# First queries and keys of heads 0 and 1 from the scale alone, with the shift added as a bias

## The chip, the cores and the metric

The kernel runs on one core of one Trainium2 chip, in one launch. The metric is the device time of that launch in microseconds (us). Three runs of the kernel before took 1315.22, 1316.06 and 1317.70 us; their median, 1316.06, is the time before.

## The reference, cut to what matters

Two layers of a diffusion backbone on 256 context tokens (`x_prompt`) and 1024 latent tokens (`x_sample`) of width 1024. Layer 0 mixes tokens by gated linear attention with 4 heads, layer 1 by softmax attention; the change touches only the beginning of layer 0:

```python
mod = silu(c) @ w_ada[0] + b_ada[0]          # c for latent tokens, c_ctx for context tokens
shift, scale, gate = split(mod, 3)            # 1024 each
h = rms_norm(x, norm_g[0]) * (1.0 + scale) + shift
proj = h @ gla_w_in                           # queries 512, keys 512, values 1024, gate 1024
q = q.reshape(..., 4 heads, 128) * 128 ** -0.5
z = (h @ wa1[d]) @ wa2[d] + ba[d]             # decay of direction d, rank 16
```

Since `h` is a scaled part plus `shift`, a product `h @ w` is the product of the scaled part plus one vector, `shift @ w`, that is the same for all latent tokens.

## The kernel before, in words

**Products and numbers.** The products of float32 numbers are made from pairs of float16 tiles: each operand is scaled by a power of two and split into a high and a low half, and three matmuls (high by high, low by high, high by low) are summed in a bank of PSUM (`mm3`, L126). A product over 1024 inputs takes eight blocks of 128, so 24 matmuls. `hT_hi` and `hT_lo` hold the modulated input with its 1024 channels as eight blocks of 128 partitions and its 1280 tokens along the free side; `whi` and `wlo` are the halves of a weight block.

**Tokens.** They come in three groups, in this order: latent tokens 0 to 511 (group 0), latent tokens 512 to 1023 (group 1), the 256 context tokens (group 2). `CHUNKS` and `GROUPS` name the same three in columns and in rows of 128.

**Set-up (L1218 to L1285).** It stands in the program in this order:
- `ada_load` (L274) loads blocks of `w_ada`, 1024 by 256 each, in two halves. Blocks 4 to 7 hold the scale, blocks 0 to 3 the shift. `gemv` (L278) multiplies a block by the condition vectors with 8 matmuls (L283), ScalarE copies the bank (L289), and `mod_sum` (L292) sums four blocks into `modT` (L303). The second four blocks land in the space of `hT_hi` and `hT_lo`, which is still free.
- `group(0)` loads the first four rows of x, squares them on ScalarE (L345) and scales them on VectorE (L348); `transpose` (L353) turns each of the eight channel blocks on TensorE, and VectorE copies them to `xT`.
- `load_qk` loads and splits the query and key weights of heads 0 and 1 (L145 is the load, into a `wst` tile).
- `affine` (L316) makes the gain `gs` and the shift `sh` with a power of two that fits both, and `inv_h`, its inverse. The power of two comes from `pow2`, which takes a maximum over all partitions by a transposing matmul (L89).
- `modulate` (L357) makes one tile of a group: ScalarE computes `h = gs*xT + sh` (L364), GpSimd rounds it to the high half (L365), VectorE subtracts for the low half (L366).
- `split_rank` (L394) scales and splits the rank weights `wa1` and `wa2`.
- For each of the three groups: load, normalise, transpose and modulate it (groups 1 and 2), then `qk_piece` (L450) for the queries and the keys of head 0, then `rank` (L430): 24 matmuls of 32 output rows (L438) that rotate through three column groups of TensorE, a copy (L443), a matmul that sums the three parts, and an eviction to `r`.

The value weights of head 0 are loaded and split after the last tile of group 1.

**The loop (`gla`, L664).** Five passes of ten slots, one slot for a token tile. In pass h a slot projects the values of head h and the output gate of head h-1, makes decays two slots ahead, and runs the products of the scan for head h; `intra`, `local` and `outer` are its parts. In head 0, `PIECES` places the queries and keys of head 1: those of group 0 in slots 4 (queries) and 5 (keys), the rest in slots 8 and 9. `filler` loads further `w_ada` blocks, one in each odd slot from slot 1, and multiplies them in the even slots; a list of jobs splits the next weights.

**The order.** Each engine runs its instructions in a fixed order. The scheduler that builds the program chooses it for each engine from a simulated timeline, from the dependences and the order of the source; `issue_after(x)` forbids an instruction to stand before x. Loads are issued by SyncE, whose queue holds at a load until the space of its target is free.

## Time and profile before

| | |
|---|---|
| median of three runs | 1316.06 us (1315.22 to 1317.70) |
| the profiled execution | 1315.01 us |
| its span, first to last instruction | 1313.2 us |
| TensorE matmul (PE) | 1224.5 us busy, 93% |
| TensorE weight load (PEld), beside PE | 796.7 us, 61% |
| VectorE (DVE) | 904.4 us, 69% |
| ScalarE (ACT) | 587.5 us, 45% |
| GpSimd (POOL) | 390.0 us, 30% |
| mean granted TensorE clock | 0.986 |
| memory read, written | 104.31 MB, 37.24 MB |

The span is what the profiler recorded of one execution; the execution's own time is 1.8 us longer. Busy shares are means over stages that differ: TensorE is at 93% over the whole, but the first fortieth of the span (33 us) is set-up, where it does little else than multiply `w_ada` blocks. In the lines of the profile, `A<-whi,cst` names the output and the inputs by the program's names; "[3.61 <-DMA whi<-in_w_ada]" after an instruction says how long its engine stood idle before it and what ended the wait. In a table of stretches each engine has its busy time and, in brackets, its count of instructions.

### The profile page before, as it was taken

The page shows a single profiled execution, that of the slowest core. Times are in us where ns is not written, and L with a number is a line of the kernel's source. Part 1 is how long each engine was busy: PE and PEld are TensorE (multiplying, and loading weights), DVE is VectorE, ACT ScalarE, POOL GpSimd, SP SyncE. Part 2 cuts the span into 40 slices and gives each one's busy share as a digit, 9 for nine tenths or more (in the row PEclk, how much of TensorE's full clock was granted, in tenths as well). Part 3 has the DMA queues.
Part 4 walks back from the last instruction along what each step waited for, and adds up shares of the span by engine and source line. Part 5 has one row for each costly group of instructions (what it writes and reads, how often), then busy time and mean ns, then how long its engine had stood idle before and what let it go on. Part 6 is the DMA issues. An engine that isn't in the chain of part 4 may idle for free. (4 is left out here: it accounts for less than half of the span.)

```text
span 1313.2 us, 22291 instructions
## 1 busy us (share of the span) xinstructions
PE 1224.5 (93%) x8107; PEld 796.7 (61%) x8107; DVE 904.4 (69%) x2072; ACT 587.5 (45%) x1431; POOL 390.0 (30%) x623
## 2 busy tenths in 40 slices
PE   4789999999999999897999998999999999989998
PEld 2347664655656556665777656767666766766444
DVE  1876768886877788746564568878657587775652
ACT  2565555655656566313343454454445454431110
POOL 2232122322422233401222544544233245423000
PEclk9899999999999999998999999999999999999999
DMA  9712555354445334678653278677947748968432
GB/s 299 244 64 70 170 184 181 111 179 146 135 145 162 108 117 144 209 179 256 148 152 108 66 181 141 135 135 138 201 93 166 149 89 143 192 134 201 175 136 79
DMA packets 344766, 199.11 MB, mean 152 GB/s; under 512 B 229406, under 2 KB 331534, under 8 KB 343376
## 3 DMA queue, kind: packets, MB, share of 16 engines
q1 hardware_dynamic: 297024, 159.67, 48.5%
q10 hardware_dynamic: 47312, 37.25, 9.1%
q8 instruction: 64, 1.05, 0.3%
q0 software_dynamic: 320, 0.77, 0.2%
q14 instruction: 46, 0.38, 0.1%
HBM read 104.31 MB, written 37.24 MB: 108 GB/s over the span
## 5 line engine op out<-in xcount | busy, mean ns | idle before, releaser
L131 PEld LDWEIGHTS <-hT_hi 128*128 128x128 f16 x1440 | 140.1, 98 | 97.8 <-issue 5.3
L131 PE MATMUL mm<-whi,hT_hi 128*128 128x512 f16 (+1 forms) x560 | 195.5, 349 | 2.6 <-DVE orsa L120 2.3
L131 PE MATMUL mm<-whi,hT_lo 128*128 128x512 f16 (+1 forms) x560 | 195.4, 349 | 0.0
L131 PE MATMUL mm<-wlo,hT_hi 128*128 128x512 f16 (+1 forms) x560 | 195.4, 349 | 0.0
L131 PEld LDWEIGHTS <-whi 128*128 128x128 f16 x1368 | 134.7, 99 | 81.0 <-issue 10.9
L131 PE MATMUL mm<-hT_hi,whi 128*128 128x256 f16 (+1 forms) x512 | 155.1, 305 | 6.0 <-POOL hT_hi L365 2.9
L1028 POOL TENSOR_SCALAR phl<-p,srec 128x1280 f16<-128x1280 f32 (+1 forms) x80 | 98.3, 1229 | 204.6 <-DVE srec L1023 91.1
L131 PE MATMUL mm<-hT_lo,whi 128*128 128x256 f16 (+1 forms) x512 | 155.5, 304 | 0.2 <-DVE hT_lo L366 0.2
L131 PE MATMUL mm<-hT_hi,wlo 128*128 128x256 f16 (+1 forms) x512 | 155.3, 304 | 0.0
L1029 DVE SCALAR_TENSOR_TENSOR phl<-p,srec,phl 128x1280 f16<-128x1280 f32 (+1 forms) x80 | 107.6, 1345 | 47.9 <-POOL phl L1028 47.6
L131 PE MATMUL mm<-PT,vh 128*128 128x256 f16 x672 | 117.6, 279 | 14.7 <-DMA PT<-phl 12.0
L999 PE MATMUL S<-kT,wst 128*128 128x512 f16 (+1 forms) x624 | 121.7, 338 | 3.8 <-ACT p L1007 3.3
L1002 DVE TENSOR_REDUCE smx<-S 128x1 f32<-128x1280 f32 (+1 forms) x80 | 101.4, 1269 | 17.8 <-PE S L999 17.5
L1007 ACT ACTIVATE p<-S,snb,sexp 128x1280 f32<-128x1280 f32 (+1 forms) x80 | 99.6, 1245 | 30.3 <-DVE phl L1029 11.4
L131 PEld LDWEIGHTS <-hT_lo 128*128 128x128 f16 x720 | 70.3, 98 | 50.3 <-issue 0.9
L131 PEld LDWEIGHTS <-wlo 128*128 128x128 f16 x720 | 70.9, 99 | 41.0 <-issue 2.9
L999 PEld LDWEIGHTS <-wst 128*128 128x128 f16 x624 | 61.0, 98 | 55.5 <-issue 4.6
L131 PE MATMUL mm<-PT,vl 128*128 128x256 f16 x336 | 93.9, 280 | 0.0
L131 PEld LDWEIGHTS <-vh 128*128 128x128 f16 x672 | 66.8, 100 | 27.5 <-issue 10.5
L131 PE MATMUL y<-whi,ogT 128*128 128x256 f16 (+1 forms) x336 | 75.0, 312 | 7.7 <-DVE xr L749 7.7
L1004 ACT ACTIVATE snb<-smx,nsexp 128x1 f32<-128x1 f32 x80 | 23.4, 293 | 130.2 <-DVE smx L1002 124.9
L153 DVE TENSOR_REDUCE wmx<-wst 128x1 f32<-128x512 f32 x104 | 64.7, 675 | 14.4 <-DMA wst<-in_gla_w_in 7.8
(337 smaller groups left out, 2552.2 us busy)
## 6 DMA issues: line engine op xcount, KB each, us to landing
wada<-in_w_ada SPq DMA_DIRECT2D x13, 1024.0 KB, 6.3
wst<-in_gla_w_in SPq DMA_DIRECT2D x12, 1024.0 KB
wst<-in_att_w_in SPq DMA_DIRECT2D x10, 1024.0 KB, 5.0
xr<-x_d SPq DMA_DIRECT2D x11, 512.0 KB
og_d<-gx ACTq DMA_DIRECT2D x40, 128.0 KB, 3.8
og_d<-og ACTq DMA_DIRECT2D x40, 128.0 KB, 2.9
wst<-og_d SPq DMA_DIRECT2D x5, 1024.0 KB
out<-xr ACTq DMA_DIRECT2D x17, 256.0 KB, 2.1
```

The costliest lines, as they stand in the source:

```text
L131: self.nc.tensor.matmul(out, a, b, start=k == 0 and j == 0, stop=k == n - 1 and j == 2)
L153: nc.vector.tensor_reduce(mx[:, j : j + 1], st[:, 2 * j : 2 * j + 2, :], AX.XY, ALU.max, apply_absolute_value=True)
L999: nc.tensor.matmul(S[:, a : a + n], x, y, start=m == 0, stop=m == 2)
L1002: last = nc.vector.tensor_reduce(mx, S, AX.X, ALU.max).ins
L1004: nc.scalar.activation(nb, mx, AF.Copy, scale=self.nsexp)
L1007: nc.scalar.activation(p, S, AF.Exp, scale=self.sexp, bias=nb, accum_out=den)
L1028: nc.gpsimd.tensor_scalar(hi, p, r, 2.0 ** 14, ALU.mult, ALU.mult)
L1029: nc.vector.scalar_tensor_tensor(lo, p, r2, hi, ALU.mult, ALU.subtract)
```

## The change

It reorders the set-up and adds a second way to make the first queries and keys.

- **Loads.** The first x group is loaded first, then the query and key weights of heads 0 and 1, then the scale blocks 4 to 7, then the shift blocks 0 to 3, two into `hT` columns 768 to 1280 and two into the space that scale blocks 4 and 5 leave.
- **Scale alone.** `affine_scale` makes a gain from the scale blocks only, with its own power of two. Group 0 is modulated with it, without a shift (`modulate` with `sh` None), and the queries and keys of heads 0 and 1 for group 0 are products of these tiles (`qk_sum`, four banks of 24 matmuls).
- **Shift as a bias.** `shift_bias` splits the shift and multiplies it with the query and key weights: 24 matmuls of 32 output rows by 512, a copy on ScalarE, four small matmuls. The evictions of the four banks add the result as a bias. Those of head 1 are kept in the tile `hold`, and GpSimd copies them to their place at slots 4 and 5 of head 0, where before they were computed.
- **Second modulation.** After the first tile pass the full gain and shift are made by `affine` as before; groups 1 and 2 use them, and group 0 is modulated a second time with them, since values, gates, rank and the later heads use the full tiles.
- **Rank.** `rank` is parted into `rank` and `rank_sum`, in the order group 1, group 0, group 2, with other banks.
- **Spaces.** The pool `ada` opens before the set-up, its first tile is `hold`, and so `filler` starts its loads at slot 7 instead of slot 1. `rows` and `wa2` take other buffers.
- **Order.** `issue_after` ties a few matmuls of the key and query products behind the small matmuls of `mod_sum`, `pow2` and `shift_bias`.

The core of the difference, with the two new functions:

```diff
+    def affine_scale(self):
+        nc = self.nc
+        g = self.t(self.p1, [P, KT, 2], F32, "ga")
+        self.gains(0, g)
+        mx = self.t(self.small, [P, 1], F32, "af_m", bufs=1)
+        nc.vector.tensor_reduce(mx, g, AX.XY, ALU.max, apply_absolute_value=True)
+        m2 = self.mulcol(mx, self.mhalf[:, 0:1], self.p1, "af_n", -64.0)
+        s, inv = self.pow2(m2)
...
+    def shift_bias(self, wq):
...
+        hi, lo = (c[:, j, :, 0:2] for j in range(2))
+        nc.scalar.activation(hi, sh, AF.Copy, scale=s)
+        nc.vector.scalar_tensor_tensor(lo, sh, s, hi, ALU.mult, ALU.subtract)
+        ps = self.bank("A")
+        for k in range(KT):
+            j = k % 4
+            for m, (x, y) in enumerate(((0, 0), (0, 1), (1, 0))):
+                last = nc.tensor.matmul(
+                    ps[32 * j : 32 * j + 32, :], c[:, x, k, :], wq[y][:, k, :], start=k < 4 and m == 0,
+                    stop=k >= 4 and m == 2, tile_position=(0, 32 * j), skip_group_check=True,
+                ).ins
+        m = self.t(self.hw, [P, 512], F32, "h32", bufs=3)
+        nc.scalar.copy(m, ps)
...
+        if self.sh is None:
+            last = nc.scalar.activation(h, xT, AF.Copy, scale=g)
...
+    def qk_piece(self, h, which, c, wq, ps=None, inv=None, bias=None):
+        if c == 0 and self.kept:
+            out = self.qkt[:, 1280 * which : 1280 * which + 512]
+            self.nc.gpsimd.tensor_copy(out, self.kept.pop(0))
...
+            xs = group(0)
+            wq = k.wtile(0)
+            for i in range(2):
+                run(k.load_qk(wq, 0, i))
...
+            k.mod_sum(parts, "cs")
+            k.gs, k.sh, k.inv_h = k.affine_scale()
             for kk in range(KT):
                 act, dve = k.modulate(xT[:, kk, :], kk, GROUPS[0][0])
...
+            with tc.issue_after(act.ins):
+                xs = group(1)
...
+            bias, b1, b2 = k.shift_bias(wq)
+            p1 = k.tick
+            pieces = [k.qk_sum(0, j, 0, wq, ties=({}, {3: m1, 11: p1, 20: b1})[j]) for j in range(2)]
...
+            for kk in range(KT):
+                act, dve = k.modulate(k.transpose(xs, kk, banks[1:][kk % 5]), kk, GROUPS[1][0])
+            pieces += [k.qk_sum(1, j, 0, wq, ("z", "mm")[j], ({3: b2}, None)[j]) for j in range(2)]
...
+            for kk in range(KT):
+                k.modulate(xT[:, kk, :], kk, GROUPS[0][0])
+            with tc.issue_after(act.ins):
+                xs = group(2)
...
-            elif queue:
+            elif queue and slot > 6:
```

**SyncE, the loads of the set-up.** In this queue before, after the small loads, the scale blocks (`whi`, `wlo`, x2 for the two halves of a block) stand ahead of the x rows, and the shift blocks (`hT_hi`, `hT_lo`) at the end, with a load of the loop's state behind them:

```order
L274 DMA whi_31_147<-in_w_ada 128x4x256 x2
L274 DMA wlo_32_148<-in_w_ada 128x4x256 x2
L274 DMA whi_37_175<-in_w_ada 128x4x256 x2
L274 DMA wlo_38_176<-in_w_ada 128x4x256 x2
L1237 DMA x_203<-in_x_sample 128x1024
L1237 DMA x_205<-in_x_sample 128x1024
L1237 DMA x_207<-in_x_sample 128x1024
L1237 DMA x_209<-in_x_sample 128x1024
L145 DMA wst_275<-in_gla_w_in 128x8x256
L145 DMA wst_304<-in_gla_w_in 128x8x256
L274 DMA hT_hi_71<-in_w_ada 128x4x256 x2
L274 DMA hT_lo_72<-in_w_ada 128x4x256 x2
```

And the same place after:

```order
L1319 DMA x_150<-in_x_sample 128x1024
L1319 DMA x_152<-in_x_sample 128x1024
L1319 DMA x_154<-in_x_sample 128x1024
L1319 DMA x_156<-in_x_sample 128x1024
L146 DMA wst_173<-in_gla_w_in 128x8x256
L146 DMA wst_202<-in_gla_w_in 128x8x256
L275 DMA whi_58_231<-in_w_ada 128x4x256 x2
L275 DMA wlo_59_232<-in_w_ada 128x4x256 x2
L275 DMA whi_60_237<-in_w_ada 128x4x256 x2
L275 DMA wlo_61_238<-in_w_ada 128x4x256 x2
L275 DMA hT_hi_71<-in_w_ada 128x4x256 x2
L275 DMA hT_lo_72<-in_w_ada 128x4x256 x2
```

The x rows and the query and key weights (`wst`) moved ahead of all of `w_ada`; the last two shift blocks, which follow the rows shown, go to `whi` and `wlo` of the first scale blocks.

**ScalarE, between the first tiles and those of group 1.** Before, the last tile of group 0 (`h` from `xT`) is followed by the squares of group 1 (`junk`), the evictions of head 0's first queries and keys (L457), the scaling of the rank weights (L403 to L410), the copy of the rank product (L443), and the first tile of group 1:

```order
L364 ACTIVATE h_110_465<-xT_224,sh_90_409,gs_89_405 128x512
L345 ACTIVATE junk_146,nt_s_136_600<-x_592 128x1024
L345 ACTIVATE junk_146,nt_s_136_600<-x_594 128x1024
L345 ACTIVATE junk_146,nt_s_136_600<-x_596 128x1024
L345 ACTIVATE junk_146,nt_s_136_600<-x_598 128x1024
L457 ACTIVATE qk_98<-mm_509,iqk_101_433 128x512
L457 ACTIVATE qk_98<-mm_535,iqk_102_435 128x512
L403 ACTIVATE wa1h_486<-wa_29_144,p2s_482 128x256
L407 ACTIVATE wa_21_128<-wa_28_142,p2s_482 98x1024
L410 ACTIVATE wa_21_128<-wa_28_142,p2s_482 1x1024
L443 COPY h_130_586<-mm_561 96x512
L364 ACTIVATE h_140_618<-z_613,sh_90_409,gs_89_405 128x512
```

After, from the last tile of the first pass on:

```order
L423 ACTIVATE h_98_406<-xT_247,gb_374 128x512
L402 ACTIVATE junk_149,nt_s_105_422<-x_414 128x1024
L402 ACTIVATE junk_149,nt_s_105_422<-x_416 128x1024
L289 COPY mod_477<-o_468 128x256
L402 ACTIVATE junk_149,nt_s_105_422<-x_418 128x1024
L402 ACTIVATE junk_149,nt_s_105_422<-x_420 128x1024
L385 ACTIVATE af_b_496<-modT_19_129 128x16
L349 ACTIVATE shc_531<-modT_19_129,p2s_527 128x8x2
L360 COPY h_138_560<-A_535 128x512
L425 ACTIVATE h_149_636<-cs_631,sh_118_493,gs_117_489 128x512
L534 ACTIVATE qk_98<-mm_575,qkb_141_569,iqa_99_410 128x512
L534 ACTIVATE qk_98<-mm_600,qkb_143_573,iqa_100_412 128x512
```

The copy of a shift block (L289), the small steps of `affine` and `shift_bias` (L385, L349) and the copy of the bias product (L360) now stand ahead of group 1's first tile; the rank weights went behind.

**TensorE, in the key product of group 0 (bank `mm_600`).** Before, the transposes of group 1's first row stand behind the whole key product (bank `mm_535`), whose last matmul is the first row here:

```order
L131 MATMUL mm_535<-hT_hi_71,wlo_60_274 128x512
L353 MATMUL z_613<-ident_79,x_592 128x128
L353 MATMUL cs_622<-ident_79,x_592 128x128
L353 MATMUL A_631<-ident_79,x_592 128x128
L353 MATMUL kt_640<-ident_79,x_592 128x128
L353 MATMUL U_649<-ident_79,x_592 128x128
```

After, eight transposes of all four rows and the two matmuls of `pow2` (L89) stand within it:

```order
L132 MATMUL mm_600<-hT_lo_72,whi_38_171 128x512
L410 MATMUL cs_631<-ident_79,x_414 128x128
L410 MATMUL U_658<-ident_79,x_414 128x128
L410 MATMUL cs_631<-ident_79,x_416 128x128
L410 MATMUL U_658<-ident_79,x_416 128x128
L410 MATMUL cs_631<-ident_79,x_418 128x128
L410 MATMUL U_658<-ident_79,x_418 128x128
L410 MATMUL cs_631<-ident_79,x_420 128x128
L410 MATMUL U_658<-ident_79,x_420 128x128
L89 LDWEIGHTS af_m_499
L89 MATMUL o_501<-ident_79,af_m_499 128x128
L89 LDWEIGHTS af_o_517
```

The key product of group 0 now waits in the queue for the normalised rows of group 1.

More of the change, by code (lines that the diff above doesn't have):

```diff
@@ L130, in mm3 @@
             for j, (a, b) in enumerate(((lh, rh), (lh, rl), (ll, rh))):
-                self.nc.tensor.matmul(out, a, b, start=k == 0 and j == 0, stop=k == n - 1 and j == 2)
+                with self.tc.issue_after(ties[3 * k + j]) if ties and 3 * k + j in ties else nullcontext():
+                    self.nc.tensor.matmul(out, a, b, start=k == 0 and j == 0, stop=k == n - 1 and j == 2)
     def hT(self, k, a, n):
@@ new lines, in shift_bias @@
+    def shift_bias(self, wq):
+        nc, p1 = self.nc, self.p1
+        sh = self.modT[0][:, 0:8, :]
+        mx = self.t(self.p1, [P, 1], F32, "af_o")
+        nc.vector.tensor_reduce(mx, sh, AX.XY, ALU.max, apply_absolute_value=True)
+        s, inv = self.pow2(mx)
+        c = self.t(p1, [P, 2, KT, 32], F16, "shc")
+        nc.gpsimd.memset(c, 0.0)
+        hi, lo = (c[:, j, :, 0:2] for j in range(2))
[8 more added lines that the diff above has]
+                    stop=k >= 4 and m == 2, tile_position=(0, 32 * j), skip_group_check=True,
+                ).ins
+        m = self.t(self.hw, [P, 512], F32, "h32", bufs=3)
+        nc.scalar.copy(m, ps)
+        ps = self.bank("kt")
+        out = []
+        for j in range(4):
+            end = nc.tensor.matmul(
+                ps[:, 2 * j : 2 * j + 2], m[:, P * j : P * j + P], self.sel[:, 0:2], start=True, stop=True
+            ).ins
+        for j in range(2):
+            t = self.mulcol(inv, wq[2][j], self.p1, f"shs{j}", [DK ** -0.5, 1.0][j])
+            o = self.t(p1, [P, 2], F32, f"qkb{j}")
+            nc.vector.tensor_scalar(
+                o, ps[:, 4 * j : 4 * j + 4].rearrange("p (h i) -> p h i", i=2)[:, :, 1], t, None, ALU.mult
+            )
+            out.append(o)
+        return out, last, end
@@ L319, in affine @@
         g = self.t(sp, [P, KT, 2], F32, f"gs{l}")
[L320 to L323 removed]
+        self.gains(l, g)
         sh = self.t(sp, [P, KT, 2], F32, f"sh{l}")
@@ new lines, in emit @@
+            free = [t[:, :, 768:1280].bitcast(F32) for t in (k.hT_hi, k.hT_lo)] + [b[2] for b in loads[0:2]]
+            shifts = [k.ada_load(0, j, t, KT // 2) for j, t in enumerate(free[0:2])]
+            xT = k.t(k.p1, [P, KT, 512], F32, "xT")
+            for kk in range(KT):
+                nc.vector.tensor_copy(xT[:, kk, :], k.transpose(xs, kk, ("z", "mm")[kk % 2]))
+            parts = [k.gemv(*b, ("A", "kt", "U", "o")[j], True) for j, b in enumerate(loads)]
+            shifts += [k.ada_load(0, 2 + j, t, KT // 2) for j, t in enumerate(free[2:])]
@@ new lines, in emit @@
+            first = dve.ins
+            with tc.issue_after(first):
+                k.split_rank(*w)
+                wv = k.wtile(1)
+                run(k.load_v(wv, 0))
+            for kk in range(KT):
+                k.modulate(xT[:, kk, :], kk, GROUPS[0][0])
+            with tc.issue_after(act.ins):
+                xs = group(2)
+            for j in range(2):
+                k.qk_piece(0, j, 1, wq)
+            r1 = k.rank(1, "z")
+            r0 = k.rank(0, "cs")
+            k.rank_sum(1, r1, "A")
@@ L1286, in emit @@
+            for kk in range(KT):
+                k.modulate(k.transpose(xs, kk, banks[2:][kk % 4]), kk, GROUPS[2][0])
+            k.qk_piece(0, 0, 2, wq)
+            k.rank_sum(0, r0, "z")
+            r2 = k.rank(2, "cs")
+            k.qk_piece(0, 1, 2, wq)
+            k.rank_sum(2, r2, "A")
         k.tl = k.pool("tl", ctx=c)
         k.spl = k.pool("spl", ctx=c)
-        k.ada = k.pool("ada", ctx=c)
         W, W2 = I["att_w_in"][0], I["att_w_out"][0]
```

123 lines of the change are left out of this document (63 added, 60 removed).

## The prediction

> **What bounds the kernel now.** I read the table of stretches first, cut where the stages change: at 54.3 us, where the first query matmul runs, at 104.3, where the first value matmul runs, and at 201, where the value tiles of head 1 begin.
>
> ```profile
> core 0: us, PE busy (x) PEld busy (x) DVE busy (x) ACT busy (x) POOL busy (x), PEclk, DMA share, GB/s
> 0.00:54.30 54.30, 27.82 (x197) 14.14 (x198) 23.09 (x65) 16.08 (x33) 7.27 (x15) 0.96 0.95 310
> 54.30:104.30 50.00, 44.06 (x277) 23.74 (x277) 37.28 (x73) 35.35 (x60) 19.09 (x27) 0.94 0.18 62
> 104.30:201.00 96.70, 94.14 (x677) 65.99 (x676) 70.20 (x176) 49.67 (x118) 22.93 (x44) 0.98 0.46 145
> ```
>
> TensorE does no projection for the first 54.3 us: DMA is the limit there (share 0.95). From 104.3 on TensorE is the limit, 94 of 96.7 us; its waits in that stretch come to one that counts:
>
> ```profile
> PE A L610 <- POOL at L556: 2.2, 1, 2.2
> ```
>
> So the change has two places to act: how late projection starts, and how much TensorE work is left after 104.3. Next, the timeline of the set-up. Weight and x blocks land in half-megabyte pieces, and four waits of TensorE on them date the 1st, 4th, 17th and 24th piece:
>
> ```profile
> 8.96 1.08 PE L283 MATMUL A<-whi,cst 128*32 128x256 f32 x8 [3.61 <-DMA whi<-in_w_ada]
> 15.61 1.08 PE L283 MATMUL kt<-wlo,cst 128*32 128x256 f32 x8 [0.43 <-DMA wlo<-in_w_ada]
> 34.43 1.08 PE L283 MATMUL A<-hT_hi,cst 128*32 128x256 f32 x8 [0.28 <-DMA hT_hi<-in_w_ada]
> 45.14 0.64 PE L283 MATMUL o<-hT_lo,cst 128*32 128x256 f32 x8 [0.17 <-DMA hT_lo<-in_w_ada]
> ```
>
> Today x is pieces 9 to 12, and what follows x is the chain that ends last: last square, normalisation, weight split, both halves of the modulation, eight modulated tiles, first query matmul.
>
> ```profile
> 27.86 1.06 ACT L345 ACTIVATE junk<-x 128x1024 f16<-128x1024 f32 x1
> 28.83 0.19 ACT L345 ACTIVATION_READ_ACCUMULATOR junk<-x 128x1 f32 x1
> 30.45 2.74 DVE L348 TENSOR_SCALAR x<-x,nt_r 128x1024 f32<-128x1024 f32 x4 [1.23 <-POOL nt_r L122]
> 50.21 0.17 DVE L303 TENSOR_TENSOR modT<-cs,cT 128x16 f32<-128x16 f32 x1
> 52.46 0.23 DVE L334 TENSOR_SCALAR gs<-gs,p2s 128x16 f32<-128x16 f32 x1
> 52.72 3.10 ACT L364 ACTIVATE h<-xT,sh,gs 128x512 f32<-128x512 f32 x4 [2.09 <-DVE gs L334]
> 54.30 1.01 PE L131 MATMUL mm<-hT_hi,whi 128*128 128x512 f16 x2 [2.92 <-POOL hT_hi L365]
> 59.82 0.81 ACT L364 ACTIVATE h<-xT,sh,gs 128x512 f32<-128x512 f32 x1 [0.68 <-DVE hT_lo L366]
> 61.91 0.69 DVE L366 TENSOR_TENSOR hT_lo<-h,hT_hi 128x512 f16<-128x512 f32 x1 [0.51 <-POOL hT_hi L365]
> ```
>
> From 30.45 to 50.21 VectorE is full, so the start of projection hangs on when x lands, not on the last w_ada block.
>
> **The change part by part.** *Start.* x becomes pieces 1 to 4, so its last row lands at 15.6 instead of behind eight pieces of w_ada. The last square ends 1.06 + 0.19 later, at 16.9; normalisation starts 1.43 after that (28.83 + 0.19 to 30.45), at 18.3; the same VectorE work as now (19.8 us) brings the scale half of modT to 38.1. Its w_ada blocks are pieces 9 to 16, in by 33 (34.43 less one step), so they do not hold it; nor does SyncE, whose last two shift loads wait for the products of the first two scale blocks (pieces 9 to 12), long done when their turn comes. From modT to the first modulated tile takes 2.5 us now (50.21 to 52.72); the new chain has about five more small VectorE steps and two ScalarE steps fewer: 2.9. First h at 41.0, first query matmul 1.6 behind it at 42.6: 11.7 us earlier.
>
> *First pass.* The tiles come at the pace of now: last h starts 7.1 after the first and takes 0.8, last hT_lo ends 9.9 after it, at 50.9. TensorE has 27 query and key matmuls and the four shift blocks (pieces 17 to 24, the last at 45.1) to do meanwhile; it follows the tiles.
>
> *The queue behind it.* On ScalarE the squares of the second x group come next, at 49.0; x is now pieces 25 to 28, and at the spacing of 17 to 24 (1.53 us) the last lands at 51.3. Four squares of 1.2 (1.06 and its 0.19, nearly end to start) and one copy of half a bank, 0.4, end at 54.2; normalisation runs 55.6 to 58.4. In TensorE's new order the transposes of this group stand in front of the second half of the key matmuls, so TensorE idles from about 54 or 56 to 58.4. The two power-of-two chains follow (reduce, cross-partition matmul, interleaved small steps, split of the shift: 3.3 us an estimate from the 2.25 that one such chain takes now, modT at 50.21 to the gains at 52.46, and the steps of the second), so the shift block starts at 61.7.
>
> *The shift block* is new: 24 matmuls of 32x512. The nearest row is the rank projection, 24 of the same size that rotate through three column groups; the other end is the plain 128x512 spacing.
>
> ```profile
> 70.83 0.39 PE L438 MATMUL mm<-hT_hi,wa1h 128*32 128x512 f16 x1 [0.28 <-ACT wa1h L403]
> 72.91 0.38 PE L438 MATMUL mm<-hT_hi,wa1l 128*32 128x512 f16 x1
> 130.98 0.38 PE L131 MATMUL mm<-hT_hi,whi 128*128 128x512 f16 x1
> 134.00 0.38 PE L131 MATMUL mm<-hT_hi,wlo 128*128 128x512 f16 x1
> 67.67 0.27 PE L353 MATMUL z<-ident,x 128*128 128x128 f32 x1
> 69.20 0.27 PE L353 MATMUL U<-ident,x 128*128 128x128 f32 x1
> 74.70 0.58 ACT L443 COPY h<-mm 96x512 f32<-96x512 f32 x1
> ```
>
> The rank block takes 2.5 us; 14 plain steps in 3.02 us are 0.216 each, and 24 of those 5.2. (The last three rows are for below: 14 transposes in 1.53 us, 0.11 each, and a copy of a bank, 0.6.) Here three matmuls in a row use one column group and the next three another, so only every third can overlap: I take 3.6, range 2.5 to 5.2. The Trainium skill, "TensorE: Matmul & The Clock Gate", Part 3 on packing, measures 2.38 times for three column tiles; by that the block would take 2.2 us and the sum would come out 1.4 lower. No row here shows a group used three times running.
>
> It ends at 65.3. ScalarE's copy of its result stands in the queue ahead of every tile of the second group, so these start at 66.0, not at 61: 5 us in which the modulation stands still, covered on TensorE by key and query work. Four small matmuls and four transposes later, at 67.3, TensorE has 93 query and key matmuls without a gap (20.1 us), 16 transposes (1.8) and two small ones: 89.6.
>
> *Second pass.* Group 0 is modulated again: eight activations, eight GpSimd copies, eight VectorE subtractions more.
>
> ```profile
> L365 POOL TENSOR_SCALAR hT_hi<-h 128x512 f16<-128x512 f32 x8 | 7.3, 923 | 24.2 <-ACT h L364 24.1
> L366 DVE TENSOR_TENSOR hT_lo<-h,hT_hi 128x512 f16<-128x512 f32 x8 | 6.8, 886 | 2.7 <-POOL hT_hi L365 2.7
> ```
>
> At 9.9 us per eight tiles it would be free beside TensorE's query and key work, but ScalarE's queue holds the first x_prompt square after its second tile, and that load waits for the last transpose of group 1 (76.5):
>
> ```profile
> x<-in_x_prompt SPq DMA_DIRECT2D x2, 512.0 KB, 4.2
> 70.06 0.17 DVE L102 TENSOR_SCALAR p2s<-p2e 128x2 int32<-128x2 int32 x1
> 93.62 0.56 ACT L364 ACTIVATE h<-z,sh,gs 128x256 f32<-128x256 f32 x1
> 99.13 0.94 DVE L366 TENSOR_TENSOR hT_lo<-h,hT_hi 128x256 f16<-128x256 f32 x2 [0.30 <-POOL hT_hi L365]
> 104.27 0.28 PE L131 MATMUL mm<-whi,hT_hi 128*128 128x256 f16 x1
> ```
>
> So the third tile starts near 82, and the six that are left end at 92 with the x_prompt normalisation among them. The scale of the rank weights, in VectorE's queue behind them, is there at 92.3 (70.06 now), the two rank blocks run 94 to 98.9 on an otherwise idle TensorE, and copy, sum and eviction put the first tile of group 2 at 101 (93.62 now). Eight tiles take 6.5 (93.62 to 100.07); the third rank block now runs between them, not behind, so the first value matmul follows at 108.0. **The set-up ends 3.7 us later than now** (104.27), having done head 1's first queries and keys as well.
>
> *Head 0.* Those 48 matmuls leave TensorE's queue at slots 4 and 5: 48 x 0.216 = 10.3 us. The evictions go too; in their place GpSimd copies two 128x512 tiles. No such copy is in the trace; the hT_hi group above, of that size, has 0.92 each. GpSimd is busy 23 of 96.7 us there: nothing if they fall in a gap (which I take), 1.8 us if a tile `at` that TensorE waits for queues behind both. The four w_ada loads and sums that start at slot 7 instead of 1 keep their cost and only move. Not all of the 10.3 comes back: VectorE has 70.2 us of work in 96.7, and in 86.4 it is at four fifths, with a weight split queued in most slots. VectorE stood on a landing and GpSimd ran long once already:
>
> ```profile
> 159.03 2.46 DVE L153 TENSOR_REDUCE wmx<-wst 128x1 f32<-128x512 f32 x4 [2.42 <-DMA wst<-in_gla_w_in]
> 164.63 3.47 POOL L556 TENSOR_TENSOR at<-am 128x128 f32<-128x128 f32 x1 [0.29 <-DVE am L554]
> ```
>
> I take 2 us of new waits of that size, range 0 to 6.
>
> Sum: +3.7 - 10.3 + 2.0 = -4.6 us. The profiled execution took 1315.0 (span 1313.2 and 1.8 around it), so it would take 1310.4; it lies 1.1 under the median of the runs, 1316.06, so the forecast for a median is **1311.5**.
>
> **The rivals.** *Head 0 is not TensorE-bound (slower).* If VectorE's and GpSimd's chain sets the slots once the 48 matmuls are gone, nothing comes back and the set-up's 3.7 is left: 1319.8. It is slower as soon as less than 1.1 of the 10.3 returns. For it: 70.2 of VectorE's 96.7, and the two rows above. Against: one wait of TensorE in that stretch. 0.18.
>
> *The clock drops (no change).* TensorE's clock was halved after it did little for some 6 us, and came back after 5.5 us of matmuls; a gap of 2 us left it whole.
>
> ```profile
> 48.00:51.00 3.00, 0.64 (x4) 0.56 (x4) 2.68 (x7) 1.69 (x4) 0.00 (x0) 0.83 0.89 311
> 51.00:54.00 3.00, 0.29 (x1) 0.13 (x2) 1.59 (x11) 1.28 (x2) 0.37 (x1) 0.50 1.05 360
> 57.00:60.00 3.00, 3.00 (x9) 1.06 (x7) 2.49 (x4) 2.12 (x4) 2.55 (x4) 0.50 0.07 19
> 60.00:63.00 3.00, 3.00 (x15) 1.27 (x13) 2.45 (x6) 2.94 (x6) 1.42 (x2) 0.97 0.00 0
> 73.00:76.00 3.00, 0.96 (x7) 0.24 (x2) 0.65 (x2) 2.42 (x4) 0.00 (x0) 1.00 0.00 0
> ```
>
> The gap before 58.4 is 2.5 to 4.5 us. If it halves the clock, 5.5 us of key and shift matmuls run at half speed, 2.75 us more, and the shift's copy holds ScalarE that much longer: -1.9, 1314.2. The Trainium skill, same page, "Why this matters for your kernels", wants no idle gap over some 3 us between bursts; the five rows agree with it, and by it this gap is on the edge. 0.17.
>
> *The set-up ends no later than now (faster by more).* If the shift block overlaps (2.5), x_prompt does not hold ScalarE and the rank blocks start as soon as the queries and keys are done, 3.7 falls away and -8.3 is left: 1307.8. For it: TensorE's own work from 42.6 on is only 14 us more than now (10.3 + 3.6) against a start 11.7 earlier. Against: three queues must all run free. 0.18.
>
> **How the numbers follow.** Forecast 0.42; the three rivals 0.18, 0.17, 0.18; 0.05 for anything outside. A measurement of this kernel tells about 0.2% from no change, 2.6 us. Faster: most of the forecast, the last rival and a little of the clock's: 0.58. Slower: head 0's rival and the tail: 0.21. Same: 0.21. The range takes the fast rival with all of head 0's 10.3 and today's 2.2 us wait gone too (-12.5: 1303.5), and head 0's rival with GpSimd's 1.8 on top (+5.5): 1321.6.
>
> **What would show it.** Right: first query matmul at 42 to 44; TensorE idle before the group-1 transposes near 58; first h of group 1 behind the shift copy near 66; first value matmul at 106 to 110; slots 4 and 5 of head 0 some 5 us shorter each. Wrong: a first query matmul after 46 (then x or the scale blocks land later than by piece count), a first value matmul before 104 or after 113, or waits of TensorE on VectorE and GpSimd of over 6 us in all between the first value matmul and head 1.

## The result, and the profile after

The changed kernel takes 1330.74 us (median of 4 runs, 1327.05 to 1331.85) against 1315.64 (4 runs, 1312.01 to 1317.70): ratio 1.0113, 95% interval 1.0083 to 1.0143. It is slower by about 15 us, where 4.6 us faster was forecast, and it lies above the range, which ended at 1321.6. Its profiled execution took 1331.85, span 1330.1.

The table of stretches, cut in both kernels at the same events: the first query matmul, the first value matmul, for each head the eviction of the next head's first value tile, and for head 3 that of its own last. First the loop of the kernel before (heads 0 to 3, and what lies behind the loop), then the whole changed kernel:

```profile
core 0: us, PE busy (x) PEld busy (x) DVE busy (x) ACT busy (x) POOL busy (x), PEclk, DMA share, GB/s
104.27:201.66 97.39, 94.83 (x681) 66.39 (x679) 70.86 (x177) 49.70 (x118) 22.96 (x44) 0.98 0.45 144
201.66:324.62 122.96, 119.01 (x683) 67.98 (x682) 92.75 (x250) 69.42 (x178) 35.79 (x59) 0.99 0.51 162
324.62:433.60 108.98, 108.98 (x612) 65.27 (x611) 87.04 (x233) 67.13 (x173) 30.92 (x55) 1.00 0.46 142
433.60:514.01 80.41, 77.78 (x423) 47.90 (x422) 68.07 (x187) 50.52 (x140) 27.03 (x51) 1.00 0.34 106
514.01:1313.20 799.19, 752.06 (x5244) 511.35 (x5242) 525.30 (x1091) 299.31 (x731) 247.00 (x374) 0.99 0.65 152
```

```profile
0.00:44.19 44.19, 22.14 (x162) 13.14 (x163) 23.32 (x66) 14.88 (x29) 7.85 (x17) 0.93 0.98 310
44.19:112.39 68.20, 62.50 (x392) 32.37 (x392) 46.96 (x105) 43.41 (x76) 24.89 (x35) 0.95 0.26 92
112.39:195.15 82.76, 78.94 (x573) 59.81 (x571) 61.39 (x154) 42.38 (x106) 21.62 (x44) 0.98 0.33 104
195.15:327.87 132.72, 121.80 (x689) 69.25 (x688) 101.85 (x269) 72.58 (x187) 33.24 (x60) 0.97 0.54 167
327.87:446.36 118.49, 115.58 (x671) 67.35 (x670) 87.48 (x235) 68.88 (x179) 29.35 (x55) 1.00 0.50 157
446.36:525.79 79.43, 77.78 (x435) 47.57 (x434) 67.23 (x187) 50.44 (x138) 30.02 (x51) 1.00 0.34 104
525.79:1330.10 804.31, 755.93 (x5228) 513.04 (x5226) 526.02 (x1092) 299.48 (x730) 247.24 (x373) 0.98 0.65 151
```

Each kernel was profiled a second time later. With both profiles of each, in us, and beside them what the prediction's sum had:

| stretch | before | after | difference of the means | predicted |
|---|---|---|---|---|
| to the first query matmul | 54.3, 54.6 | 44.2, 42.4 | -11.2 | -11.7 |
| to the first value matmul | 50.0, 50.0 | 68.2, 68.9 | +18.6 | +15.4 |
| head 0 | 97.4, 95.7 | 82.8, 80.7 | -14.8 | -8.3 |
| head 1 | 123.0, 121.1 | 132.7, 135.4 | +12.0 | 0 |
| head 2 | 109.0, 108.9 | 118.5, 120.4 | +10.5 | 0 |
| head 3 | 80.4, 80.9 | 79.4, 80.6 | -0.6 | 0 |
| behind the loop | 799.2, 796.2 | 804.3, 800.6 | +4.8 | 0 |

The table shows where to look. The start went as told, the way to the first value matmul took 3.2 us more, and head 0 gained 6.5 more (three `w_ada` blocks have left it too). Heads 1 and 2, of which the prediction said nothing, lost 22 us.

The set-up, in the timeline of the changed kernel (start, duration, engine, instruction, idle time before it and what ended it):

```profile
37.71 1.71 PE L302 MATMUL cs<-sel,mod 128*128 128x2 f32 x8 [2.20 <-ACT mod L289]
39.45 0.17 DVE L306 TENSOR_TENSOR modT<-cs,cT 128x16 f32<-128x16 f32 x1 [0.21 <-PE cs L302]
44.19 1.01 PE L132 MATMUL mm<-hT_hi,whi 128*128 128x512 f16 x2
58.44 0.33 PE L410 MATMUL cs<-ident,x 128*128 128x128 f32 x1 [0.23 <-DVE x L405]
62.51 0.42 PE L355 MATMUL A<-whi,shc 128*32 128x512 f16 x4
63.95 0.39 PE L132 MATMUL mm<-hT_hi,wlo 128*128 128x512 f16 x1
64.63 0.78 ACT L425 ACTIVATE h<-cs,sh,gs 128x512 f32<-128x512 f32 x1
92.10 0.51 ACT L464 ACTIVATE wa1h<-wa,p2s 128x256 f16<-128x256 f32 x1 [1.63 <-DVE p2s L102]
101.27 0.56 ACT L425 ACTIVATE h<-A,sh,gs 128x256 f32<-128x256 f32 x1 [0.42 <-PE A L410]
112.39 0.27 PE L132 MATMUL mm<-whi,hT_hi 128*128 128x256 f16 x1
```

modT stands at 39.45 (38.1 told), the first query matmul at 44.2 (42.6), the first tile of group 1 at 64.63 (66.0), the scale of the rank weights at 92.1 (92.3), the first tile of group 2 at 101.27 (101). Only the last row, the first value matmul at 112.4, is far off (108.0).

In head 1, one chain shows what was new. VectorE waits for the landing of a weight block; what is queued behind that wait is late, and TensorE stands:

```profile
233.41 2.46 DVE L154 TENSOR_REDUCE wmx<-wst 128x1 f32<-128x512 f32 x4 [2.18 <-DMA wst<-in_gla_w_in]
237.92 1.22 PE L646 MATMUL U<-v,ks 128*128 128x256 f32 x2 [4.69 <-DVE Wa L673]
```

### The profile page after: what moved, and what is told of

It reads as the page before. It is cut to its first block, busy times and chain, and to the rows that moved or that the text cites. A ratio compares the mean times of both kernels' runs of the same rounds, so it can differ in the third digit from the quotient of the medians.

```text
span 1330.1 us, 22417 instructions
## 1 busy us (share of the span) xinstructions
PE 1234.7 (93%) x8141; PEld 802.5 (60%) x8141; DVE 914.2 (69%) x2105; ACT 592.0 (45%) x1441; POOL 394.2 (30%) x634
## 5 line engine op out<-in xcount | busy, mean ns | idle before, releaser
L132 PE MATMUL mm<-hT_hi,whi 128*128 128x256 f16 (+1 forms) x504 | 151.2, 300 | 2.1 <-DMA whi<-w_g 1.4
L132 PE MATMUL mm<-hT_lo,whi 128*128 128x256 f16 (+1 forms) x504 | 151.1, 300 | 0.0
L132 PE MATMUL mm<-hT_hi,wlo 128*128 128x256 f16 (+1 forms) x504 | 150.6, 299 | 0.0
L1109 DVE SCALAR_TENSOR_TENSOR phl<-p,srec,phl 128x1280 f16<-128x1280 f32 (+1 forms) x80 | 107.7, 1346 | 51.4 <-POOL phl L1108 50.8
L154 DVE TENSOR_REDUCE wmx<-wst 128x1 f32<-128x512 f32 x104 | 64.5, 677 | 27.0 <-DMA wst<-in_gla_w_in 13.8
L1084 ACT ACTIVATE snb<-smx,nsexp 128x1 f32<-128x1 f32 x80 | 23.4, 293 | 130.8 <-DVE smx L1082 125.6
```

The lines of the kernel that those rows point to most:

```text
L132: self.nc.tensor.matmul(out, a, b, start=k == 0 and j == 0, stop=k == n - 1 and j == 2)
L154: nc.vector.tensor_reduce(mx[:, j : j + 1], st[:, 2 * j : 2 * j + 2, :], AX.XY, ALU.max, apply_absolute_value=True)
L1084: nc.scalar.activation(nb, mx, AF.Copy, scale=self.nsexp)
L1109: nc.vector.scalar_tensor_tensor(lo, p, r2, hi, ALU.mult, ALU.subtract)
```

## The experiments

The suspects were the `w_ada` loads of the loop, which the change starts at slot 7 (theory A), and a loop that gives nothing back when matmuls leave it (theory B). Ratios are to the kernel before on the same chip, which took 1311.8 to 1314.8 in the five sets of runs; prices are taken from the ratios, and the quotient of two medians can differ from them by 0.3%.

**late_ada** (edit on the kernel before):

```diff
-            elif queue:
+            elif queue and slot > 6:
```

> The kernel before with one line changed: the loads of w_ada in the loop start at slot 7 instead of slot 1, as in the changed kernel. Theory A (the moved loads): the loop of the changed kernel idles 10 us more because these loads, and the products and sums behind them, fall together with the weight loads of heads 1 and 2, for which VectorE waits 12 us more. Then this line alone makes the kernel before 6 to 12 us slower, lost between slots 10 and 30. Theory B (no work to hide behind): once the 48 matmuls are out of head 0, the chain of weight loads and splits sets the pace of the loop, whatever w_ada does. Then this line changes nothing: within 2 us of before.

1326.39 us, ratio 1.0088 (1.0060 to 1.0115). One line of the change, alone, costs 11.5 us, so theory B, by which it would cost nothing, does not explain this loss. Heads 0 to 2 in its profile:

```profile
104.79:200.25 95.46, 88.91 (x619) 64.17 (x617) 67.49 (x170) 46.13 (x110) 21.95 (x43) 0.96 0.36 111
200.25:325.84 125.59, 119.45 (x689) 67.70 (x688) 94.84 (x253) 70.39 (x183) 35.71 (x60) 1.00 0.51 161
325.84:443.45 117.61, 115.87 (x671) 67.34 (x670) 87.22 (x234) 68.98 (x180) 30.43 (x55) 1.00 0.50 158
```

Its timeline has one wait late in head 0:

```profile
178.47 0.58 PE L131 MATMUL mm<-hT_hi,whi 128*128 128x512 f16 x1 [4.15 <-DVE s L312]
```

62 matmuls left head 0 (619 against 681; 48 of them are the products of three blocks) and it became only 1.9 us shorter: TensorE waited 4.15 us for a bank that the sum of a `w_ada` block still held, since the sum (L312) stood late in VectorE's queue, and the clock fell behind that. Head 2, where TensorE was busy all the time before (108.98 of 108.98 us), got 59 matmuls and became 8.6 longer.

**start_only** (edit on the changed kernel: no kept tiles, loads from slot 1):

```diff
-        k.hold = k.t(k.ada, [P, KT, 256], F32, "wada").rearrange("p k n -> p (k n)")
...
-            pieces += [k.qk_sum(1, j, 0, wq, ("z", "mm")[j], ({3: b2}, None)[j]) for j in range(2)]
...
-            elif queue and slot > 6:
+            elif queue:
```

> The changed kernel without head 1's part: head 1's queries and keys of group 0 are computed at slots 4 and 5 again, nothing is kept, and the w_ada loads start at slot 1 as before. The early start, the bias and the second modulation stay. Set-up: the 48 matmuls (10.3 us) fall out of it, but the rank chain waits for the second modulation, not for them, so the first value matmul comes at 105 to 110, not at 102. Theories A and B both leave the loop as in the kernel before; the time is then that of before plus 1 to 6 us.

1314.29 us, ratio 0.9994 (0.9974 to 1.0014). First value matmul at 109.3, as told, though the 48 matmuls are gone from the set-up.

**start_late_ada** (start_only with `elif queue and slot > 6:`):

> The same as the run before it, with the w_ada loads starting at slot 7. Theory A: 6 to 12 us slower than with the loads from slot 1. Theory B: the same within 2 us.

1324.02 us, ratio 1.0076 (1.0047 to 1.0106): again some 10 us. Its profile does not show where they lie: the profiled execution was the shortest of seven, 1317.10, with a span of 1315.3 against 1314.9 in start_only. In it head 0 is 6.6 us shorter than in start_only (88.8 against 95.4) and head 2 is 6.4 longer (115.1 against 108.7). In start_only TensorE is busy in head 0 for 95.2 of 95.4 us, and there the blocks were not free.

**rank_early** (edit on the changed kernel):

```diff
-            with tc.issue_after(first):
-                k.split_rank(*w)
...
+            with tc.issue_after(b2):
+                k.split_rank(*w)
             for kk in range(KT):
                 act, dve = k.modulate(k.transpose(xs, kk, banks[1:][kk % 5]), kk, GROUPS[1][0])
```

> The changed kernel with the scaling and splitting of the rank weights moved in the source ahead of group 1's tiles, so that VectorE does it before the second modulation and not behind it. If that queue is what makes the set-up end late, the 3.5 us wait of TensorE behind 88.5 and the drop of the clock behind it go, the first value matmul comes 4 to 6 us earlier than in the changed kernel (112.4), and the time is 4 to 6 us lower (1325 to 1327). If group 2's own work sets the end, it stays within 1.5 us.

1328.75 us, ratio 1.0113 (1.0076 to 1.0150); first value matmul at 112.7. Inconclusive: the tie named a TensorE instruction, and VectorE's two maxima of the rank weights moved ahead of the first query matmul (one stands at 30.72, in the changed kernel at 81.5), which then came at 47.3. It is mended below (start_rank).

**query_kept** (start_only with head 1's first queries, not its keys, made in the set-up; a 2 KB tile of their own):

```diff
+        k.hold = k.t(k.pool("hold", ctx=c), [P, 512], F32, "hold")
...
+            pieces.append(k.qk_sum(1, 0, 0, wq, "z", {3: b2}))
+            nc.scalar.activation(k.hold, pieces[2], AF.Identity, scale=inv0[0], bias=bias[0][:, 1:2])
+            k.kept.append(k.hold)
```

> The changed kernel with half of head 1's part: its first queries are made in the set-up and kept, its first keys are computed at slot 5 again. The kept tile has a space of its own, so the w_ada loads start at slot 1 as before. Against the run without head 1's part (start_only, 1314.3): 24 matmuls fewer in head 0 (5.2 us); in the set-up half of the 3.1 us that separate the first value matmul there (109.3) and in the changed kernel (112.4). Theory A (all loss is in the moved w_ada loads): 1309 to 1312. Theory B (nothing comes back when matmuls leave head 0): 1315 to 1317.

1313.43 us, ratio 0.9990 (0.9966 to 1.0015). Head 0 took 91.3 and head 1 121.4, against means of 96.5 and 122.0 before: these 24 matmuls did come back whole, 5.3 us, which speaks against B. The longer set-up took it away again (first value matmul at 112.0, 104.3 before).

**full_early** (edit on the changed kernel: two loads into the weight space that is empty until slot 4):

```diff
-            elif queue and slot > 6:
-                held.append(k.ada_load(*queue.pop(0), k.t(k.ada, [P, KT, 256], F32, "wada")))
+            elif queue and slot != 5:
+                if slot == 1:
+                    w2[:] = [x.rearrange("p k n -> p (k n)").bitcast(F32).rearrange("p (k n) -> p k n", n=256) for x in k.wtile(2)[0:2]]
+                to = w2.pop() if slot < 5 else k.t(k.ada, [P, KT, 256], F32, "wada")
+                held.append(k.ada_load(*queue.pop(0), to))
```

> The whole change, with the w_ada loads at slots 1 and 3 again: these two blocks go to the weight space that stands empty until slot 4; the load at slot 5 is left out, so the last of the ten comes at slot 21, not at 25 as in the changed kernel, nor at 19 as before. Theory A: the 10 us return for the most part, and the saving of head 0 shows: 1307 to 1313. Theory B: over 1320.

1317.51 us, ratio 1.0019 (0.9995 to 1.0043). Most of the loss is gone, yet no gain shows.

**before_catch_up** and **catch_up** (late_ada and the changed kernel, one block in every slot from 7 on; the edit of the first):

```diff
-            elif slot % 2 == 0:
+            elif slot > 6:
                 if held:
                     part.append(k.gemv(*held.pop()))
-            elif queue:
-                held.append(k.ada_load(*queue.pop(0), k.t(k.ada, [P, KT, 256], F32, "wada")))
+                if queue:
+                    held.append(k.ada_load(*queue.pop(0), k.t(k.ada, [P, KT, 256], F32, "wada")))
```

> The kernel before with the w_ada loads starting at slot 7, as in late_ada (1326.4), but one block in every slot instead of every second, so that the last is multiplied at slot 17 and none in head 2. Theory A1: the price of the late start is paid in head 2, where TensorE has no idle time and gets the products, and in the stages whose order they shift; then it goes: 1311 to 1316. Theory A2: the price comes from loads of w_ada that meet the weight loads of heads 0 and 1; then it grows or stays, with one block per slot: 1322 or more.

> The whole change with the w_ada loads starting at slot 7, one block in every slot, so that the last is multiplied at slot 17. Theory A1: 1307 to 1313, faster than the kernel before. Theory A2: 1322 or more.

1324.87 (1.0103, 1.0079 to 1.0126) and 1329.18 (1.0133, 1.0108 to 1.0158): A1 falls in its time, since the price did not go. But heads 1 and 2 of before_catch_up show it to have moved with the products, not with the loads:

```profile
200.46:334.51 134.05, 125.77 (x741) 70.00 (x740) 92.73 (x254) 69.74 (x181) 35.16 (x60) 0.99 0.55 173
334.51:442.42 107.91, 107.61 (x592) 64.84 (x591) 88.41 (x235) 65.81 (x173) 29.68 (x55) 1.00 0.43 133
```

Head 2 lost a block and is 1.1 us shorter than before; head 1 got 58 matmuls and is 11 longer. From this theory C: a block costs next to nothing in head 0, and its price wherever TensorE is full. The two runs that test it against A2 (the bytes of the loads):

**full_on_time** (full_early with loads at slots 1, 3, 6, 7, 9, ... 19):

```diff
+                if held and (slot % 2 == 0 or slot == 7):
+                    part.append(k.gemv(*held.pop()))
+                if queue and (slot == 6 or slot % 2 == 1 and slot != 5):
...
```

> The whole change with the w_ada loads at slots 1, 3, 6 and then every odd slot from 7, so that the last comes at slot 19, as in the kernel before. Theory C: a w_ada block costs little in head 0, where the pace of the slots is not set by TensorE alone, and its full price in heads 1 and 2: in head 2, where TensorE is busy all the time, the eight kernels so far take 107.5 us plus about 2.4 us for every block multiplied there. Then head 2 takes 109 to 110 here (111.2 in full_early, 118.5 in the changed kernel) and the time is 1311 to 1316, 2 us below full_early. If the start alone counts, whatever the end, it is that of full_early, 1317.5 within 1.5.

**late_small_loads** (late_ada with an eighth of each block):

```diff
+        if small:
+            self.nc.sync.dma_start(to[:, 0:1], src[:, 0:1])
+            return l, b, to[:, 0:1].to_broadcast([P, KT, 256])
...
```

> late_ada (the kernel before with the w_ada loads from slot 7) with an eighth of each of the ten blocks loaded, and this eighth multiplied eight times: the products, copies and sums are the same in number and place, but the bytes of the loads are an eighth. It leaves seven eighths of these weights out. Theory A2 (loads that meet the weight loads): the 11.5 us of late_ada go, 1313 to 1316, and head 2 is back at 109. Theory C (TensorE work put where TensorE is full): head 2 stays at 115 to 118 and the time at 1322 to 1326.

Head 2 of full_on_time, with the products where they were before, and of late_small_loads, with an eighth of the bytes:

```profile
327.26:436.19 108.93, 108.93 (x612) 65.24 (x611) 88.22 (x235) 67.45 (x173) 31.21 (x55) 1.00 0.46 142
```

```profile
326.52:445.97 119.45, 117.61 (x671) 67.91 (x670) 87.38 (x235) 68.83 (x179) 30.65 (x55) 0.99 0.43 133
```

The price does not hang on the bytes: late_small_loads took 1328.54 (1.0129, 1.0104 to 1.0153) and A2 falls. The length of head 2 follows its matmuls. But full_on_time took 1323.97 (1.0080, 1.0050 to 1.0110), not 1311 to 1316: C prices head 2 and does not explain that time. In its profile head 1 (126.8), the set-up (first value matmul at 113.4) and the stretch behind the loop (804.4) are long.

Head 2 in the kernels so far, by TensorE's matmuls in it:

| matmuls | length of head 2, us |
|---|---|
| 592 (before_catch_up, catch_up) | 107.9, 107.4 |
| 608 (start_only, query_kept) | 108.7, 108.7 |
| 612 (before twice, full_on_time) | 109.0, 108.9, 108.9 |
| 635 (full_early) | 111.2 |
| 667 (start_late_ada) | 115.1 |
| 671 (late_ada, late_small_loads, rank_early, after twice) | 117.6, 119.5, 119.7, 118.5, 120.4 |

The step is more than the engine time of the added matmuls. In head 2 of late_ada a block's products run 1.0 us (326.39 to 327.39) and its sum 0.4 to 0.5 (376.81 to 377.18, 334.17 to 334.69), so three blocks hold TensorE for 4 to 5 us, and head 2 grew by 8.6. TensorE stands 1.7 us there that it did not stand before; the rest is not explained, nor the spread among the kernels with 671.

**before_again, after_again, query_kept_again** (no edit, a second profile):

> The kernel before, unchanged, for a second profile. The stages behind the loop took 799.2 us in the first profile and 804.3 in that of the changed kernel, in which nothing of them is changed. If that difference is scatter between executions, this profile lies some 3 us or more from 799.2; if it belongs to the two programs, it lies within 1.5 of 799.2.

> The changed kernel, unchanged, for a second profile. As for the run before: behind the loop 804.3 within 1.5 us if the difference belongs to the program, 3 us or more away from it if it is scatter.

> query_kept, unchanged, for a second profile: behind the loop 803.7 us in the first, 795.3 in start_only, 799.2 and 796.2 in the kernel before. If keeping tiles lengthens these stages, it is over 802 again; if it is scatter, anywhere from 795 to 804.

1309.10, 1330.76 and 1309.54 us. Behind the loop: 796.2 and 800.6; the two profiles of query_kept differ most:

```profile
514.23:1317.90 803.67, 755.26 (x5244) 512.22 (x5242) 518.80 (x1091) 300.35 (x731) 251.64 (x374) 0.98 0.65 151
```

```profile
513.27:1307.40 794.13, 749.18 (x5244) 509.67 (x5242) 519.41 (x1091) 300.27 (x731) 250.61 (x374) 0.99 0.66 153
```

One program, 9.5 us apart: single profiles say nothing on a few microseconds there.

**start_rank, query_rank, full_rank** (start_only, query_kept, full_early with the rank weights split behind the split of the shift, tied to a VectorE instruction):

```diff
+        self.split_lo = nc.vector.scalar_tensor_tensor(lo, sh, s, hi, ALU.mult, ALU.subtract).ins
...
+            with tc.issue_after(k.split_lo):
+                k.split_rank(*w)
```

> start_only (no kept tiles, w_ada from slot 1) with the rank weights scaled and split by VectorE right behind the split of the shift, ahead of group 1's tiles and of the second modulation. In start_only TensorE stands from 79 to 88 waiting for small steps that lie in VectorE's queue behind the second modulation, and the clock is halved from 83 to 94 (3.7 us lost). If that queue sets the end of the set-up where the 48 matmuls are absent, the first value matmul comes at 102 to 105 instead of 109.3, and the time is 4 to 7 us under start_only: 1307 to 1311, below the kernel before. If group 2's x load and its tiles set it, it stays within 2 us of start_only (1314).

> The same edit on query_kept (head 1's first queries kept, keys at slot 5, w_ada from slot 1). There TensorE idled from 80 to 88 as well, and the clock was halved from 84 to 95. First value matmul at 105 to 108 instead of 112.0 if the queue sets it; time 1307 to 1311 against 1313.4.

> The same edit on full_early (the whole change, w_ada at slots 1 and 3). Here TensorE has the 48 matmuls to do meanwhile, so 1 to 3 us in the first value matmul (110.0 there), and 1314 to 1317 against 1317.5. If this is still above start_rank, keeping head 1's tiles does not pay on this kernel.

First value matmul at 106.6 (109.3 without the edit), 107.7 (112.0) and 105.3 (110.0). What goes is TensorE's wait for small VectorE steps, here in the timeline of start_only:

```profile
81.72 0.22 PE L89 MATMUL o<-ident,wm 128*128 128x128 bf16 x1 [2.03 <-DVE p2m L94]
87.76 0.61 PE L499 MATMUL z<-hT_hi,wa1h 128*32 128x512 f16 x1 [2.28 <-ACT wa1h L464]
```

The stretch from the first query matmul to the first value matmul, in start_only and then in start_rank:

```profile
43.87:109.31 65.44, 56.34 (x344) 26.94 (x344) 46.82 (x105) 42.19 (x74) 23.85 (x35) 0.88 0.27 94
```

```profile
44.02:106.59 62.57, 58.14 (x343) 27.34 (x343) 46.75 (x102) 39.93 (x68) 25.07 (x34) 0.87 0.29 100
```

The times: 1311.84 (1.0003, 0.9989 to 1.0017), 1317.13 (1.0040, 1.0026 to 1.0054), 1312.68 (1.0014, 0.9994 to 1.0033). VectorE's queue does set part of the set-up's end, in full_rank also with the 48 matmuls present, where less was expected. The total gains less than the set-up, and query_rank is even slower than query_kept: its head 1 took 126.6 against 121.4.

**full_old_slots, full_rank_old_slots** (full_early and full_rank with all loads in their old slots):

```diff
-    {4: [(0, 0)], 5: [(1, 0)], 8: [(0, 1)], 9: [(1, 1), (0, 2), (1, 2)]},
+    {4: [(0, 0), (1, 0)], 8: [(0, 1)], 9: [(1, 1), (0, 2), (1, 2)]},
...
-            elif queue and slot != 5:
+            elif queue:
```

> The whole change with all ten w_ada loads in the slots of the kernel before (1, 3, 5, ... 19): the first two go to the empty weight space, and both kept tiles are copied at slot 4, so that the third finds its space free. Theory C: head 2 takes 109 (111.2 in full_early, 119.4 in the changed kernel), heads 0 and 1 as in full_early, 85 and 126. If the stages behind the loop take what they take in the kernel before (797) and not what the profiles with moved loads show (802 to 805), the time is 1308 to 1312; if they stay long, 1314 to 1318.

> The same with the rank weights split early, as in full_rank (1312.7; loop's end at 505.7 in its profile, 513 in the kernel before). First value matmul at 105 to 106, head 2 at 109; time 1304 to 1308, 0.3 to 0.6% under the kernel before, if the stages behind the loop take 797; 1310 to 1314 if they stay at 802 or more.

1318.50 (1.0038, 1.0016 to 1.0059) and 1312.75 (1.0001, 0.9985 to 1.0018). Heads 0 to 2 of full_rank_old_slots:

```profile
107.36:191.73 84.37, 83.83 (x633) 61.47 (x631) 63.69 (x163) 43.89 (x112) 24.99 (x45) 1.00 0.37 117
191.73:321.78 130.05, 121.15 (x686) 68.28 (x685) 98.28 (x264) 72.14 (x184) 36.02 (x59) 0.99 0.55 170
321.78:431.76 109.98, 109.39 (x611) 65.21 (x610) 87.69 (x235) 66.98 (x174) 33.72 (x55) 1.00 0.45 139
```

Head 2 is back at 110 and head 0 at 84.4, 12 less than before; head 1 takes 130, 8 more, with as many matmuls (686 against 683). In full_old_slots the stretch behind the loop took 795.9, as in the kernel before, for which 1308 to 1312 had been told; 1318.50 misses that. Its profiled execution took 1314.58, near the shortest of twelve, so what the median has more is not in view. No version beats the kernel before; the best ones equal it.

## Why the prediction was wrong

*The step that failed* is the sentence in "Head 0": "The four w_ada loads and sums that start at slot 7 instead of 1 keep their cost and only move." Their cost did not stay the same: the late start alone costs 11.5 us on the kernel before, and 10 on start_only. All ten blocks move three places back, so the products of three leave head 0 and those of three more fall into head 2. In head 0 of the kernel before they were nearly free: late_ada took 62 matmuls out of it and gained 1.9 us. In head 2 TensorE is busy all the time, and 59 matmuls more cost 8.6 there in late_ada, 10.5 in the changed kernel. With an eighth of the bytes the price did not fall (late_small_loads, ratio 1.0129 against 1.0088).

*The second loss is head 1*, +12.0, and its cause is open. 3.6 of it appear in late_ada too (125.6 against 122.0). The runs do not part the rest between the late loads and the short head 0. With the first loads at slots 1 and 3 and a head 0 nearly as short (84.9 to 87.0), head 1 is only 3 to 5 us longer than before (125.2 in full_rank, 125.8 in full_early, 126.8 in full_on_time). With all loads in their old slots it is 8 longer (130.4 and 130.1). With half of head 1's tiles kept it is not longer in query_kept (121.4) and 4.6 longer in query_rank (126.6).

Weight splits did move from head 0 to head 1. VectorE takes four maxima (L153 before, L154 after) of each landed weight block: 28 in head 0 and 28 in head 1 before, 20 and 36 in the changed kernel, so two blocks moved; in full_early one (24 and 32). Its waits for landing weights in head 1 (us in total, times, the longest), before and in the changed kernel:

```profile
DVE wmx L153 <- DMA wst<-in_gla_w_in: 5.4, 3, 2.1
DVE wmx L153 <- DMA wst<-in_att_w_in: 2.2, 1, 2.2
```

```profile
DVE wmx L154 <- DMA wst<-in_gla_w_in: 8.5, 4, 3.0
DVE wmx L154 <- DMA wst<-in_att_w_in: 6.5, 4, 2.9
```

7.6 us became 15.0, and 13.1 in full_rank_old_slots. That these waits make head 1 long is read from the chain shown above, not tried by taking them away, and their sum alone does not set its length: start_only has 11.5 us of them in a head 1 of 125.4. The rival "head 0 is not TensorE-bound" named this mechanism and put it a head too early: in head 0 all 10.3 us came back (84.7 in full_old_slots, with as many blocks in it as before, against 96.5).

*The start* was right: -11.2 against -11.7. x did land early, and VectorE's work set the rest.

*The shift block* was mis-sized: 24 matmuls from 62.51 to 63.95, 1.44 us where 3.6 was taken (2.5 to 5.2). The premise, three matmuls running in one column group, is the order of the source. In the trace they start in fours, one round every 0.216 us, high halves of the weights, then low, then high twice:

```profile
62.74 0.41 PE L355 MATMUL A<-wlo,shc 128*32 128x512 f16 x4
62.95 0.63 PE L355 MATMUL A<-whi,shc 128*32 128x512 f16 x8
```

At the plain spacing of 0.216 the 24 would take 5.2, so the four column groups ran 3.6 times as fast. The Trainium skill, "TensorE: Matmul & The Clock Gate", Part 3 on packing, has 2.38 times for three column tiles, and an estimate from that is 2.2 us. This block, over four, was faster, and the measurement decides.

*The idle gap before group 1's transposes* was not there: TensorE waited 0.2 us at a time (58.44), and the clock stayed whole, so that rival did not come true at its place. It did elsewhere: the clock was halved from 37.91 to 48.15, where the kernel before has the same from 49.96 to 60.2, and from 92.52 to 95.94, behind a pause of TensorE from 88.7 to 92.4 that holds one matmul. The kernel before has nothing like the second, which costs up to 1.7 us. The dates told up to 101.27 were met all the same.

*The end of the set-up* was mis-sized by one term. Up to group 2's first tile (101.27) every date above is right within 2 us; from there to the first value matmul it took 11.1 us, where 7.0 was told. The kernel before takes 10.7 for the same (93.62 to 104.27), so nothing was saved there. The prediction let the third rank block run between the query and key matmuls at no cost. In the kernel before it ran in one piece behind them, and its 24 matmuls started within 0.8 us (101.88 to 102.66). In the changed kernel TensorE has no pause from 102.2 on, and the block is cut into 12 pieces of one to three matmuls. Each piece takes 0.42 us from the matmul before it to the one behind it, where two query or key matmuls in a row are 0.11 apart (of the three rank matmuls the last is shown):

```profile
104.47 0.27 PE L132 MATMUL mm<-hT_hi,wlo 128*128 128x256 f16 x1
104.58 0.27 PE L132 MATMUL mm<-hT_hi,whi 128*128 128x256 f16 x1
104.79 0.28 PE L499 MATMUL cs<-hT_hi,wa1l 128*32 128x256 f16 x1
105.00 0.28 PE L132 MATMUL mm<-hT_lo,whi 128*128 128x256 f16 x1
```

Twelve times 0.31 is 3.7 us, most of the 4.1; no run left the block in one piece. The wait for the rank weights behind the second modulation, which the prediction named, was worth 2.7 to 4.7 us when it was taken away.

*The forecast's frame* was wrong as well: it let TensorE work that leaves a stage count in full, and looked for new waits only in that stage. With the old slots and the rank weights split early (full_rank_old_slots) the change comes out at no difference.

*Open:* the stretch behind the loop is 4.8 us longer in the means of two profiles, yet one program alone differed by 9.5. full_rank ends its loop at 505.7, some 7 us before the kernel before (514.0 and 511.1), and its time shows none of it. Which part of that belongs to the programs is not settled.

## What to carry to other kernels

Work that fills idle time is priced by the stage into which it falls: before a buffer's new use pushes background loads and products later, look up which engine is full there. Three blocks whose absence gave back 1.9 us in a stage with slack cost 8.6 in a full one. Look also at what a shortened stage leaves undone for the next one; here weight splits moved on, though what that cost is not settled. Keep narrow matmuls in one run, and do not mix them among full ones. And when one line of a large change looks like bookkeeping, run the kernel before with that line alone: it told most here.

## What the runs showed of the hardware

**The clock.** PEclk at the very start of a view is no reading: the trace's first record of the clock stands at 39.72 us in the kernel before and at 31.08 in the changed one, and ahead of it the views print 1.00. The pace shows otherwise. In the kernel before the same eight products took 1.08 us at 34.43 and 0.64 at 45.14 (the prediction shows both rows), and in the changed one 1.08 at 24.43 and 0.61 at 34.90: TensorE ran slower until that record.

From there on the granted clock changes in steps of 3.41 us. TensorE alone, in stretches of that grid in the changed kernel (length, PE busy, granted clock, DMA share, GB/s):

```profile
34.50:37.91 3.41, 1.21 (x22) 1.00 1.10 350
37.91:48.15 10.24, 10.17 (x60) 0.50 1.07 372
89.11:92.52 3.41, 0.35 (x2) 1.00 0.00 0
92.52:95.94 3.42, 3.42 (x24) 0.50 0.00 0
379.24:382.65 3.41, 1.60 (x11) 1.00 0.20 60
382.65:386.06 3.41, 3.41 (x18) 1.00 0.79 235
```

In the two profiles of each kernel, up to 560 us, the clock was halved 16 times. Ahead of 15 of them TensorE was busy for 0 to 0.49 of a step, ahead of one for 0.63; the emptiest steps that left the clock whole had 0.47 to 0.49. So in these traces about half a step of work decides, and not the length of one gap. The Trainium skill, same page, "Why this matters for your kernels", wants gaps of no more than some 3 us; here a halving (at 174.44 in the changed kernel) had no longer gap ahead of it than 2.03 us, and a gap of 2.04 us (at 73.29 in the kernel before) left the clock whole.

**Narrow matmuls.** Matmuls of 32 output rows, started in fours over four column groups, ran 3.6 times as fast as plain ones. Put between plain matmuls of 256 columns, a piece of one to three of them cost 0.31 us beyond the plain step of 0.11.
